# Row scales spread through memory, gates cumulated by a scan: a two-layer hybrid decoder on one core

## The chip, the core and the metric

The kernel runs on one core of a Trainium2 chip. The core's engines work side by side, each through its own list of instructions in order, and wait for each other on semaphores: TensorE (PE: matrix products and transposes into PSUM), VectorE (DVE), ScalarE (ACT), GpSimd (POOL) and SyncE (SP, which here only issues transfers). Transfers (DMA) are issued by SP, ACT or POOL and carried out by 16 DMA engines that these queues share. The metric is the device time of one execution in microseconds; lower is better.

## The reference

Two layers act on x of 256 rows by 1024. Each has three sub-layers, each with an RMS norm ahead and one behind it:

```python
def rms_norm(x, g):
    y = x * lax.rsqrt(jnp.mean(x * x, axis=-1, keepdims=True) + EPS)
    return y * g

for l in range(DEPTH):                          # 2
    h = rms_norm(x, pre_mix_g[l])
    x = x + rms_norm(parallel_mixer(h, ...), post_mix_g[l])
    h = rms_norm(x, pre_cross_g[l])
    x = x + rms_norm(memory_cross_attention(h, mem_n, ...), post_cross_g[l])
    h = rms_norm(x, pre_ffn_g[l])
    x = x + rms_norm((silu(h @ w_gate) * (h @ w_up)) @ w_down, post_ffn_g[l])
```

The mixer projects h by w_in (1024 x 3080) and gives the columns to three groups of heads: an RG-LRU (a gated linear recurrence), a forgetting attention (FoX, 8 heads) and a retention (4 heads). Of the FoX group this matters here: each head has a gate per row, and the logits take differences of the gates' running sum.

```python
log_f = jax.nn.log_sigmoid(f_logit + b_f)       # (rows, 8)
c = jnp.cumsum(log_f, axis=1).transpose(0, 2, 1)
logits = q @ k.T * scale + c[..., None] - c[:, :, None, :]
```

Cross-attention goes from the rows to 256 memory rows; the FFN is 2816 wide.

## The kernel before

The 256 rows are two tiles of 128 (`NT = 2`). Weights come in pieces of 512 KB: SP loads a piece into one of five `raw` buffers, ScalarE rounds it to `hi`, VectorE forms the rest `lo` = raw - hi, and PE computes every product three times (hi by hi, hi by lo, lo by hi). A raw buffer is free for the next load when `lo` is done. VectorE and ScalarE do this among their other work, in order.

A norm's gain goes into the transposed activations `xt` at once, but its 1 / rms (`rstd`, one number per row, computed on GpSimd as a power) is applied only to the products. Where a product has the rows on partitions, that is a scale per partition. Where it is transposed (columns on partitions, rows along the free axis: the mixer's `lru` and `fk` projections and the FFN's `gate` and `up`), the 256 numbers have to stand on every partition. The function `spread` makes this tile, `rsb`, once per mixer and once per FFN, four times in all: VectorE scales the identity by `rstd` (`diag`), PE multiplies a matrix of ones by that, ScalarE copies the result from PSUM. The users read `got["rs"]`: `lxp`, `lyT` and two `kT` in a mixer, the `fs` of nine pieces in an FFN.

In `gates`, the log gates `lf` (128 rows by 8, from a `softplus` on VectorE) are cumulated along the rows by three products with a triangle `tri` and with ones; the result `cT` (8 x 256) is written to memory by GpSimd's queue and read back four times, spread over all partitions (`far`).

Order: the kernel's code runs against a planner (`Flow`) with cost figures and a clock for each engine. Tasks are Python generators; a task that yields a tile goes on when the planner's PE clock has passed the time at which the tile is ready by its figures. So the order of each engine's instructions is fixed when the program is built, and a transfer's latency in the figures moves whatever waits for its tile to a later place in the lists. GpSimd's list holds, besides transfers (`PO.dma_start`: mask, constants, memory rows `msrc`, `cum`, `far`, and the post-norm gains `gpost`), the powers for the norms and, in layer 0, a chain of some 30 small operations for the rotary tables (`ang`). From these VectorE and ScalarE make `cs` and `c`, PE transposes them into `turn`, and the retention's `rot` needs `turn`.

The first FFN piece (`first`) has rows on partitions: gate, up, a product `fg` on VectorE, transposes on PE (`flip`), then the spread. The later pieces (`hidden`) are transposed ones. `summed` projects one piece into `fs`.

Of the kernel before, what the change touches and what calls it, by code (L numbers as in the profile page):

```python
# [10 lines left out]
F32 = mybir.dt.float32  # L11
# [4 lines left out]
ALU = mybir.AluOpType  # L16
AX = mybir.AxisListType.X

P = 128
D = 1024  # L20
KC = D // P
SEQ = 256
NT = SEQ // P
# [98 lines left out]
def _size(ap):  # L122
    return int(np.prod(ap.shape[1:]))
# [163 lines left out]
def decoder(ctx: ExitStack, tc: tile.TileContext, a, out):  # L287
    nc = tc.nc
    flow = Flow()
    V, S, PO = Engine(nc.vector, "DVE", flow), Engine(nc.scalar, "ACT", flow), Engine(nc.gpsimd, "POOL", flow)  # L290
# [6 lines left out]
    dp = ctx.enter_context(tc.tile_pool(name="dram", bufs=1, space=bass.MemoryType.DRAM))  # L297
# [5 lines left out]
    def nm(s):  # L303
        uid[0] += 1
        return f"{s}{uid[0]}"

    def work(shape, dt=F32, n="w"):
        return kp.tile(shape, dt, tag="w", name=nm(n), bufs=WORK_BUFS)
# [4 lines left out]
    def bank(n="ps"):  # L313
        return pp.tile([P, 512], F32, tag="ps", name=nm(n))
# [4 lines left out]
    def matmul(out_ap, lhsT, rhs, start, stop):  # L319
        nc.tensor.matmul(out_ap, lhsT, rhs, start=start, stop=stop)  # L320
        n = _size(out_ap)
        if lhsT.dtype == F32:
            cost = 2 * max(0.112, n / 1200.0 + 0.0025)
        elif lhsT.dtype == F32R:
            cost = max(0.119, n * 0.4475e-3 + 0.0025)
        else:
            cost = n / 2400.0 + 0.0025
        if lhsT.shape[0] == HD or out_ap.shape[0] == HD:
            cost *= 0.5
        elif lhsT.shape[0] == 32:  # L330
            cost *= 0.25
        flow.issue("PE", cost * flow.slow(), [out_ap], [lhsT, rhs])
# [6 lines left out]
    def transpose(out_ap, src):  # L339
        k = src.shape[0]  # L340
        nc.tensor.transpose(out_ap, src, ident[0:k, 0:k])  # L341
        flow.issue("PE", 0.109 * flow.slow(), [out_ap], [src])
# [37 lines left out]
    def half(ap, c):  # L380
        return ap[:, SEQ * c:SEQ * c + SEQ]

    def halves(ap, n=2):
        return ap.rearrange("p (c i) -> p c i", c=n)

    def transposes(src_list):

        b = bank("tr")
        for j, s in enumerate(src_list):
            transpose(b[0:s.shape[-1], j * P:(j + 1) * P], s)  # L390
        return b
# [25 lines left out]
    for l in range(DEPTH):  # L417
        b = {}
# [20 lines left out]
        for c in range(FB):  # L439
            c0, n = (0, 512) if c == 0 else (512 + SEQ * (c - 1), SEQ)  # L440
# [68 lines left out]
    def project(x, b):  # L509

        q = bank("acc")
        for k in range(KC):
            wh, wl = weights(b, k, NT)
            mm3(q[:, 0:b.n], x[0][:, k, :], x[1][:, k, :], wh, wl, k == 0, k == KC - 1)
            flow.tick()
        return q
# [17 lines left out]
    def project_w(x, b, c):  # L534


        q = bank("acc")
        for k in range(KC):
            wh, wl = weights(b, k, 2, slice(P * c, P * c + P))
            both = lambda: matmul(q.rearrange("p (s t i) -> p s t i", s=2, t=NT), wh, x[:, :, :, k, :], k == 0, k == KC - 1)  # L540
            if k == 0:
                both()
            matmul(halves(half(q, 0)), wl, x[:, 0, :, k, :], False, False)
            if k > 0:
                both()
            flow.tick()
        return q
# [14 lines left out]
    ident, tri, ones = (cst[:, c:c + P] for c in (C_ID, C_TRI, C_ONE))  # L562
# [213 lines left out]
    def spread(xt, got):  # L776

        while not all(n.scaled for n in xt):
            yield 0.3
        yield [n.rs for n in xt]  # L780
        d = work([P, NT, P], n="diag")
        for t in range(NT):
            V.tensor_scalar(d[:, t, :], ident, xt[t].rs, None, op0=ALU.mult)
        yield d
        b = bank("rsb")
        matmul(half(b, 0), ones, d.rearrange("p t i -> p (t i)"), True, True)
        rb = work([P, SEQ], n="rsb")
        S.copy(rb, half(b, 0))
        yield rb
        got["rs"] = rb  # L790

    def mixer(l, xt, blk, skew, between=None):
        mt = mixed()
        got = {}
        v = [work([P, 512], n="fv") for _ in range(NT)]
        rs = [None] * NT
# [4 lines left out]
        lf = [lfs[:, 4 + 8 * t:12 + 8 * t] for t in range(NT)]  # L801
# [24 lines left out]
        def gates():  # L826


            yield list(lf)
            b = bank("cum")  # L830
            matmul(b[0:8, 0:P], lf[0], tri, True, True)
            matmul(b[0:8, P:SEQ], lf[0], ones, True, False)
            matmul(b[0:8, P:SEQ], lf[1], tri, False, True)
            cT = work([8, SEQ], n="cT")
            V.tensor_copy(cT, b[0:8, 0:SEQ])
            yield cT
            dr = dp.tile([8, SEQ], F32, tag="cum", name=nm("cum"), bufs=2)
            PO.dma_start(out=dr, in_=cT)
            yield dr
            for e in range(2):  # L840
                for g in range(2):
                    far[e, g] = work([P, 2, SEQ], n="far")
                    PO.dma_start(out=far[e, g], in_=dr[4 * e + 2 * g:4 * e + 2 * g + 2, :].partition_broadcast(P))
            got["far"] = 1
# [266 lines left out]
    def parts(src, n):  # L1111

        h, l = work([P, 512], F32R, n=n + "h"), work([P, 512], F32R, n=n + "l")
        split(h, l, src)
        return h, l
# [63 lines left out]
    def ffn(xt, blk, make_post):  # L1179


        gt, got = {}, {}
        dn = [[None] * 2 for _ in range(NT)]

        def first():
            for t in range(NT):
                flow.need(lambda: xt[t].done)
                qg = project(xt[t].x, blk["gate", 0])
                tg, gg = work([P, 512], n="ft"), work([P, 512], n="fg")
                S.activation(tg, qg, AF.Tanh, bias=0.0, scale=xt[t].by[0.5])  # L1190
                V.scalar_tensor_tensor(gg, tg, 1.0, qg, op0=ALU.add, op1=ALU.mult)
                qu = project(xt[t].x, blk["up", 0])
                V.scalar_tensor_tensor(gg, gg, xt[t].rs, qu, op0=ALU.mult, op1=ALU.mult)
                flow.spawn(flip(t, gg), gg)
            flow.spawn(spread(xt, got))

        def flip(t, gg):
            tb = transposes([gg[:, j * P:(j + 1) * P] for j in range(4)])
            h, l = parts(tb, "g")
            for k in range(4):  # L1200
                gt[t, k] = tuple(x[:, k * P:(k + 1) * P] for x in (h, l))
            return
            yield

        def summed(b):

            w = work([P, 512], n="fs")
            for c in range(2):
                q = project_w(xt_all[2], b, c)
                S.copy(half(w, c), half(q, 1))  # L1210
                V.tensor_tensor(half(w, c), half(q, 0), half(w, c), op=ALU.add)
            return w

        def hidden(c):
            gs, tg = summed(blk["gate", c]), work([P, 512], n="ft")
            flow.need(lambda: "rs" in got)
            V.tensor_tensor(halves(gs), halves(gs), got["rs"].unsqueeze(1).to_broadcast([P, 2, SEQ]), op=ALU.mult)
            S.activation(tg, gs, AF.Tanh, bias=0.0, scale=0.5)
            V.scalar_tensor_tensor(gs, tg, 1.0, gs, op0=ALU.add, op1=ALU.mult)
            us = summed(blk["up", c])  # L1220
            V.tensor_tensor(gs, gs, us, op=ALU.mult)
            h, l = parts(gs, "g")
            for t in range(NT):
                for k in range(2):
                    o = SEQ * k + P * t
                    gt[t, 4 + 2 * (c - 1) + k] = tuple(x[:, o:o + P] for x in (h, l))

        def step(t, k, cc):
            if k == 0:
                dn[t][cc] = bank("dn")  # L1230
            flow.need(lambda: (t, k) in gt)
            wh, wl = weights(blk["down", k], 0, 2 * NT, slice(512 * cc, 512 * cc + 512))
            mm3(dn[t][cc], gt[t, k][0], gt[t, k][1], wh, wl, k == 0, k == FK - 1)
            flow.tick()

        first()
        spare.extend(range(NT))
        for c in range(1, FB):
            if c == FB - 1:
                spawn_post = make_post()  # L1240
            hidden(c)
            for k in blk["down_at", c]:
                for t in range(NT):
                    for cc in range(2):
                        step(t, k, cc)
        late = blk["down_at", FB]
        for t in range(NT):
            for k, cc in order(late):
                step(t, k, cc)
            spawn_post(t, dn[t], xt[t])  # L1250
        del spare[:]
# [66 lines left out]
    for l in range(DEPTH):  # L1318
        b = blks[l]
# [46 lines left out]
```

## Time and profile before

| | |
|---|---|
| median of 3 runs | 832.49 us (831.71 to 832.66) |
| the profiled execution, its own time | 832.4 us |
| its span in the trace | 830.6 us |
| granted TensorE clock | 0.998 |
| DVE, ACT, POOL busy | 71%, 54%, 10% |
| weights' queue q1 | 138.17 MB, 52.1% of the DMA engines' time |
| GpSimd's queue q0 | 7.91 MB, 2.8% |

A row of the timeline has the start, the duration, the engine, line and operation, the tile written and the tiles read (without buffer numbers) and a count; in brackets stands how long the engine had been idle before, and who ended that. Nearly all instructions carry the line of a helper (L242, L320), so they are told apart by tiles. A row of the chain that ended last has start, duration and what. Matmuls overlap, so their durations add up to more than the time; starts tell the time that each takes. A row of the table by stretches has the stretch, the sum of busy time, busy time and count of PE, PEld (weight loads), DVE, ACT and POOL, then the granted clock, the share in which the DMA engines were busy, and GB/s.

### The profile page before, as it was taken

Reading aid. Unit: us, or ns where it says so; the run is one execution under the profiler, and the core shown is the slowest. Engines: PE = TensorE matmul, PEld = TensorE weight load, DVE = VectorE, ACT = ScalarE, POOL = GpSimd, SP = SyncE. Lnnn points to the kernel's source line nnn. Section 1 sums busy time; section 2 is a strip of 40 time slices with the busy share of each in tenths; the row PEclk is TensorE's granted clock in tenths of the full one; section 3 lists DMA queues with packets and bytes.
Section 4 is the critical chain, followed back from the end, with each engine's and each line's share of the span. In section 5 each row is a group of like instructions: output and inputs, shape, how many; then the busy total and the mean of one; then the engine's idle time right before and its main releaser. Section 6 shows DMA issues by size and latency. Waiting matters only on the chain.

```text
span 830.6 us, 12999 instructions
## 1 busy us (share of the span) xinstructions
PE 818.8 (99%) x5023; PEld 714.9 (86%) x5023; DVE 588.9 (71%) x854; ACT 450.6 (54%) x728; POOL 80.2 (10%) x136
## 2 busy tenths in 40 slices
PE   9989999999999999999999999999999999999996
PEld 6989977998888888888889998789988788888885
DVE  6578996867577766758678888566767775857663
ACT  5569465746366544645474376555545563554541
POOL 2752100200020000000041100010002000000000
PEclk9999999999999999999999999999999999999999
DMA  8883545563357846557447563446444765647411
GB/s 296 305 260 121 171 158 155 188 216 114 121 185 240 251 138 220 186 157 232 137 128 237 168 204 127 151 129 228 145 129 133 232 222 181 207 147 244 139 49 51
DMA packets 101885, 147.50 MB, mean 178 GB/s; under 512 B 4976, under 2 KB 79104, under 8 KB 101696
## 3 DMA queue, kind: packets, MB, share of 16 engines
q1 hardware_dynamic: 99040, 138.17, 52.1%
q0 software_dynamic: 2080, 7.91, 2.8%
q8 instruction: 39, 0.64, 0.3%
q10 hardware_dynamic: 704, 0.59, 0.2%
q14 instruction: 22, 0.18, 0.1%
HBM read 145.59 MB, written 1.06 MB: 177 GB/s over the span
## 4 chain that ended last, share of the span: by engine, by line
PE 89%; DMA 3%; POOL 2%; issue 2%; DVE 2%; ACT 1%; DVEq 0%; POOLq 0%; ACTq 0%
PE acc L320 55%; PE dn L320 25%; PE tr L341 3%; DMA raw<-in_w_in 2%; PE co L320 1%; PE clg L320 1%; DMA raw<-in_w_down 1%; PE lg L320 1%; ACT hi L242 1%; POOL ang L242 1%; PE fo L320 1%; DVE lo L242 1%; PE ry L320 1%; POOL f L242 0%; PE gate L320 0%
## 5 line engine op out<-in xcount | busy, mean ns | idle before, releaser
L242 DVE TENSOR_TENSOR lo<-raw,hi 128x1024 fp32r<-128x1024 f32 (+2 forms) x246 | 293.9, 1215 | 88.1 <-ACT hi L242 86.7
L320 PE MATMUL acc<-xt,hi 128*128 128x256 f32 (+1 forms) x1344 | 340.1, 332 | 0.0
L242 ACT CAST hi<-raw 128x1024 fp32r<-128x1024 f32 (+2 forms) x246 | 251.9, 1043 | 92.5 <-PE acc L320 59.8
L320 PE MATMUL acc<-xt,lo 128*128 128x256 f32 x960 | 259.1, 282 | 0.0
L320 PEld LDWEIGHTS acc<-xt,hi 128*128 128x128 f32 x1344 | 223.3, 189 | 20.9 <-issue 0.4
L320 PEld LDWEIGHTS acc<-xt,lo 128*128 128x128 f32 x960 | 181.2, 189 | 6.3
L320 PE MATMUL acc<-hi,xt 128*128 128x512 f32 (+2 forms) x320 | 83.6, 351 | 0.0
L320 PEld LDWEIGHTS acc<-hi,xt 128*128 128x128 f32 x320 | 56.1, 188 | 8.5 <-ACT hi L242 0.6
L242 POOL TENSOR_TENSOR rp<-ssp,mh 128x1 f32<-128x1 f32 x12 | 6.8, 567 | 573.1 <-DVE ssp L242 573.0
L320 PE MATMUL acc<-lo,xt 128*128 128x512 f32 (+2 forms) x160 | 54.1, 349 | 0.0
L320 PE MATMUL dn<-hi,mth 128*128 128x512 f32 x128 | 51.6, 403 | 0.0
L242 DVE TENSOR_TENSOR fs<-acc,fs 128x256 f32<-128x256 f32 x72 | 30.1, 418 | 29.0 <-ACT fs L242 29.0
L320 PE MATMUL dn<-hi,mtl 128*128 128x512 f32 x128 | 50.5, 394 | 0.0
L320 PE MATMUL dn<-lo,mth 128*128 128x512 f32 x128 | 50.5, 394 | 0.0
L320 PE MATMUL acc<-mem,hi 128*128 128x256 f32 x256 | 47.3, 285 | 0.0
L242 ACT COPY fs<-acc 128x256 f32<-128x256 f32 x72 | 26.2, 364 | 37.7 <-PE acc L320 37.7
L320 PE MATMUL acc<-hi,mem 128*128 128x512 f32 x128 | 45.1, 405 | 0.0
L320 PE MATMUL dn<-hi,gh 128*128 128x512 f32 x112 | 44.3, 396 | 0.0
L320 PE MATMUL dn<-hi,gl 128*128 128x512 f32 x112 | 44.2, 394 | 0.0
L320 PE MATMUL dn<-lo,gh 128*128 128x512 f32 x112 | 44.2, 394 | 0.0
L320 PEld LDWEIGHTS acc<-mem,hi 128*128 128x128 f32 x256 | 39.5, 189 | 1.4 <-issue 1.0
L242 DVE TENSOR_TENSOR y<-dn,gpost 128x512 f32<-128x512 f32 x24 | 16.4, 685 | 28.3 <-ACT junk L242 28.3
(206 smaller groups left out, 1168.7 us busy)
## 6 DMA issues: line engine op xcount, KB each, us to landing
raw<-in_w_gate SPq DMA_DIRECT2D x44, 512.0 KB, 4.8
raw<-in_w_up SPq DMA_DIRECT2D x44, 512.0 KB, 4.6
raw<-in_w_down SPq DMA_DIRECT2D x44, 512.0 KB, 4.7
raw<-in_w_in SPq DMA_DIRECT2D x42, 512.0 KB, 5.4
raw<-in_w_ck SPq DMA_DIRECT2D x16, 512.0 KB, 3.7
raw<-in_w_cv SPq DMA_DIRECT2D x16, 512.0 KB, 4.9
raw<-in_w_out SPq DMA_DIRECT2D x16, 512.0 KB, 4.1
raw<-in_w_cq SPq DMA_DIRECT2D x16, 512.0 KB, 4.5
```

Source lines behind the costliest of these rows:

```text
L242: fn(*args, **kw)
L320: nc.tensor.matmul(out_ap, lhsT, rhs, start=start, stop=stop)
L341: nc.tensor.transpose(out_ap, src, ident[0:k, 0:k])
```

## The change

1. `spread`: each row tile's `rstd` (128 numbers of 4 bytes) is written to a tile `rs` in memory by GpSimd's queue, and one more transfer of that queue reads the 256 numbers back for every partition. `diag`, the product and the copy go.
2. `gates`: two transposes bring `lf` to 8 x 256 in PSUM, and a scan on VectorE over them with a tile of ones gives `cT`. The three products and the copy go.
3. `hidden`: where `rs` is not there yet by the planner, the `up` product is taken ahead of the gate's scaling.

```diff
@@ spread
-        d = work([P, NT, P], n="diag")
+        dr = dp.tile([NT * P, 1], F32, tag="rs", name=nm("rs"), bufs=2)
         for t in range(NT):
-            V.tensor_scalar(d[:, t, :], ident, xt[t].rs, None, op0=ALU.mult)
-        yield d
-        b = bank("rsb")
-        matmul(half(b, 0), ones, d.rearrange("p t i -> p (t i)"), True, True)
+            PO.dma_start(out=dr[t * P:(t + 1) * P, :], in_=xt[t].rs)
+        yield dr
         rb = work([P, SEQ], n="rsb")
-        S.copy(rb, half(b, 0))
+        PO.dma_start(out=rb, in_=dr[:, 0].partition_broadcast(P))
         yield rb
         got["rs"] = rb
@@ gates
             yield list(lf)
-            b = bank("cum")
-            matmul(b[0:8, 0:P], lf[0], tri, True, True)
-            matmul(b[0:8, P:SEQ], lf[0], ones, True, False)
-            matmul(b[0:8, P:SEQ], lf[1], tri, False, True)
-            cT = work([8, SEQ], n="cT")
-            V.tensor_copy(cT, b[0:8, 0:SEQ])
+            b = transposes(lf)
+            cT, one = work([8, SEQ], n="cT"), work([8, SEQ], n="one")
+            V.memset(one, 1.0)
+            V.tensor_tensor_scan(cT, one, b[0:8, 0:SEQ], 0.0, op0=ALU.mult, op1=ALU.add)
             yield cT
@@ hidden
             gs, tg = summed(blk["gate", c]), work([P, 512], n="ft")
+            us = None if "rs" in got else summed(blk["up", c])
             flow.need(lambda: "rs" in got)
...
-            us = summed(blk["up", c])
+            us = us or summed(blk["up", c])
             V.tensor_tensor(gs, gs, us, op=ALU.mult)
```

Three places in the lists, where the prediction's steps rest. First VectorE in layer 0, behind the softplus (`lo` is a weight piece, `lxp` and `lyT` use `rsb`, `ang` starts the end of the rotary tables). Before:

```order
L242 TENSOR_TENSOR lxp_647<-acc_584,rsb_528 128x2x256
L242 TENSOR_TENSOR lo_674<-raw_500,hi_673 128x1024
L242 COPY cT_681<-cum_677 8x256
L242 TENSOR_TENSOR lo_695<-raw_524,hi_694 128x1024
L242 TENSOR_TENSOR lo_712<-raw_557,hi_711 128x1024
L242 TENSOR_TENSOR lo_728<-raw_609,hi_727 128x1024
L242 TENSOR_TENSOR lyT_648<-acc_651,rsb_528 128x512
L242 TENSOR_TENSOR lo_757<-raw_645,hi_756 128x1024
L242 SCALAR_TENSOR_TENSOR ang_229<-ang_228 128x64
```

and now (the row of `cT` is the scan):

```order
L242 SCALAR_TENSOR_TENSOR cT_666<-one_667,tr_663 8x256
L242 TENSOR_TENSOR lo_686<-raw_524,hi_685 128x1024
L242 TENSOR_TENSOR lo_703<-raw_553,hi_702 128x1024
L242 TENSOR_TENSOR lo_721<-raw_603,hi_720 128x1024
L242 TENSOR_TENSOR lo_744<-raw_639,hi_743 128x1024
L242 MEMSET lxp_782 128x2x3
L242 TENSOR_TENSOR lxp_782<-acc_578,rsb_706 128x2x256
L242 TENSOR_TENSOR lyT_783<-acc_641,rsb_706 128x512
L242 TENSOR_TENSOR lo_800<-raw_655,hi_799 128x1024
L242 TENSOR_TENSOR mem_104<-xg_774,mem_104 128x512
L242 SCALAR_TENSOR_TENSOR ang_229<-ang_228 128x64
```

`lxp` moved behind two more `lo`, right ahead of `lyT`, and a part of `mem` (the memory's norm) came in ahead of `ang`.

Second GpSimd at the same time (`spl` ends its wait for the softplus, `ss` and `rstd` are the first memory tile's norm). Now:

```order
L242 TENSOR_SCALAR spl_81<-soft_83 128x4 x2
L242 TENSOR_SCALAR ang_230<-ang_226 128x64
L242 TENSOR_TENSOR ang_228<-ang_228,ang_230 128x64
L242 TENSOR_SCALAR ss_671<-ss_671 128x1
L242 TENSOR_TENSOR rstd_670<-ss_671,mh_78 128x1
L242 TENSOR_SCALAR ang_230<-ang_227 128x64
L242 TENSOR_TENSOR ang_228<-ang_228,ang_230 128x64
L237 DMA rsb_706<-rs_444 128x256
L242 TENSOR_SCALAR ang_230<-ang_226 128x64
L242 TENSOR_TENSOR ang_228<-ang_228,ang_230 128x64
L237 DMA cum_738<-cT_666 8x256
```

The read of `rsb` is new in it; the two writes of `rs` stand ahead of `spl`, and one pair of `ang` operations that was ahead of `spl` is now behind it.

Third GpSimd between the cross-attention and the FFN of layer 0 (`eps` is the last operation of the second row tile's norm). Now:

```order
L242 TENSOR_SCALAR eps_2825<-ss_2818 128x1
L237 DMA rs_2959<-rstd_2649 128x1
L237 DMA rs_2959<-rstd_2752 128x1
L237 DMA rsb_2980<-rs_2959 128x256
L237 DMA gpost_4165<-in_post_ffn_g 128x1024
```

Before, `gpost` stood right behind `eps`; now the three transfers of the spread stand between them. Layer 1 has the same.

## Prediction

> **What bounds the kernel.** I read the page's totals first, then the list of waits of TensorE (engine, tile and line that waited, for whom, us in total, times, longest), then the chain that ended last and the timeline at the places which the list names.
>
> ```profile
> span 830.6 us, 12999 instructions
> PE 818.8 (99%) x5023; PEld 714.9 (86%) x5023; DVE 588.9 (71%) x854; ACT 450.6 (54%) x728; POOL 80.2 (10%) x136
> ```
> ```profile
> PE cum L320 <- DVE hb L242: 1.5, 1, 1.5
> PE tr L341 <- DVE fg L242: 1.4, 2, 0.8
> PE warm L320 <- DVE warm L242: 1.2, 1, 1.2
> PE tr L341 <- DVE c L242: 1.0, 1, 1.0
> PE tr L341 <- ACT msrc L242: 0.4, 1, 0.4
> ```
>
> TensorE (PE) is busy 99% of the span, and all its waits for other engines are five kinds, 5.5 us. So a product taken from PE is worth its own time, except ahead of one of these waits: there PE only arrives sooner and waits longer. Three waits stand in layer 0 (cum, msrc, c), two in the heads of the FFNs (fg). The change touches both places.
>
> **Price of the removed products.** On PE's timeline I take start to start, since matmuls overlap.
>
> ```profile
> 34.83 0.28 PE L320 MATMUL acc<-xt,lo 128*128 128x256 f32 x1
> 34.95 0.60 PE L320 MATMUL rsb<-diag,cst 128*128 128x256 f32 x2
> 35.62 0.28 PE L320 MATMUL acc<-xt,lo 128*128 128x256 f32 x1
> ```
> ```profile
> 445.04 0.28 PE L320 MATMUL acc<-xt,lo 128*128 128x256 f32 x1
> 445.40 0.28 PE L320 MATMUL acc<-xt,lo 128*128 128x256 f32 x1
> 445.61 0.82 PE L320 MATMUL cum<-cst,soft 128*8 128x128 f32 x6
> 446.70 0.27 PE L320 MATMUL acc<-xt,lo 128*128 128x256 f32 x1
> ```
> ```profile
> 258.61 0.66 PE L341 MATMUL tr<-cst,fg 128*128 128x128 f32 x4 [0.60 <-DVE fg L242]
> 259.10 0.66 PE L320 MATMUL rsb<-diag,cst 128*128 128x256 f32 x2
> 259.72 0.39 PE L320 MATMUL acc<-xt,hi 128*128 128x512 f32 x1
> ```
> ```profile
> 69.94 0.44 PE tr L341 x4
> ```
>
> Three matmuls of 256 columns take 445.40 - 445.04 = 0.36 us, 0.12 each. The spread in a mixer costs 35.62 - 34.83 - 0.36 = 0.43 us. In the FFN the next "hi" would start one 0.12 us matmul after 259.10 and starts at 259.72: 0.50 us. The cumulation costs 446.70 - 445.40 - 0.36 = 0.94 us; two transposes at 0.44 / 4 each are 0.22, so 0.72 us is saved.
>
> Layer 1's mixer has no PE wait: gain 0.43 + 0.72 = 1.15 us. (GpSimd's wait for rs there holds only cum's write, which waits for cT anyway.) Both FFNs: 2 x 0.50 = 1.00 us.
>
> VectorE and ScalarE lose two diag scalings and a copy per spread; VectorE swaps a copy for a memset and a scan:
>
> ```profile
> L242 DVE COPY cT<-cum x2: 404/404/405, 51.6 to 447.7; 8x256 f32<-8x256 f32 x2
> L242 DVE TENSOR_TENSOR_SCAN ld<-t,li x4: 664/672/683, 93.8 to 494.5; 128x256 f32<-128x256 f32 x4
> ```
>
> A scan of 256 costs 0.27 us more than the copy, twice. I cost all this at nothing: these engines are 29% and 46% idle, and what waits for cT are far's loads, which the attention uses only after four more projections. Were that cover gone it would be 0.5 us.
>
> **Layer 0: three fixed times.** Here PE's gains are pinned.
>
> ```profile
> 47.70 0.81 PE L320 MATMUL cum<-cst,soft 128*8 128x128 f32 x6 [1.46 <-DVE hb L242]
> 48.79 0.28 PE L320 MATMUL acc<-xt,lo 128*128 128x256 f32 x1
> ```
> ```profile
> 54.41 0.57 POOL L242 TENSOR_TENSOR rstd<-ss,mh 128x1 f32<-128x1 f32 x1
> ```
> ```profile
> 56.22 0.66 PE L341 MATMUL tr<-cst,msrc 128*128 128x128 f32 x4 [0.36 <-ACT msrc L242]
> ```
> ```profile
> 57.13 1.23 DVE L242 TENSOR_TENSOR lo<-raw,hi 128x1024 fp32r<-128x1024 f32 x1 [2.90 <-ACT hi L242]
> 58.27 0.68 DVE L242 TENSOR_TENSOR lyT<-acc,rsb 128x512 f32<-128x512 f32 x1
> 60.22 0.22 DVE L242 SCALAR_TENSOR_TENSOR ang<-ang 128x64 f32<-128x64 f32 x1
> 60.99 0.50 DVE L242 COPY c<-cs 128x256 f32<-128x256 f32 x2 [0.32 <-ACT cs L242]
> ```
> ```profile
> 61.43 0.63 PE tr L341 x4
> ```
>
> The 0.43 us ahead of 47.70 goes into the wait for the softplus. From there PE is faster (0.22 us for 48.79 - 47.70 less two matmuls, 0.85), but the msrc transposes wait for GpSimd's rstd (ends 54.98) and ScalarE behind it, which the change does not move: still 56.22, with three matmuls fewer done (the order leaves 57 behind the cumulation instead of 60).
>
> Then the turn transposes. GpSimd issues the read of rsb two small operations after that rstd, at about 55.9. Its landing is unknown. The views of three tiles that go through the same queue, cT's write (8 KB), far's reads (256 KB each) and msrc's (512 KB), end with this row, and the list of DMA issues has posi's:
>
> ```profile
> DMA to landing us min/median/max: 2.3/3.2/4.0
> ```
> ```profile
> DMA to landing us min/median/max: 3.8/5.1/6.5
> ```
> ```profile
> DMA to landing us min/median/max: 7.6/8.8/10.1
> ```
> ```profile
> posi<-in_positions ACTq DMA_DIRECT2D x1, 1.0 KB, 5.3
> ```
>
> rsb has 128 KB of 1 KB rows, between cT's write and far's reads, and the DMA engines are busy here, so I take cT's 4.0 us: rsb lands at 59.9. VectorE has finished its two "lo" (57.13 plus 2 x 1.15, from the start-to-start step) at 59.4, so it waits 0.5 us in lxp; behind it in the order are lyT, a "lo" and a part of mem, 0.6 + 0.6 + 1.15 + 0.6, and only then ang: 62.85 instead of 60.22. c follows 0.77 and the transposes 0.44 later: 64.05. PE gets there at 56.22 + 0.44 + 21 x 0.12 + 0.44 + 33 x 0.12 = 63.6. So it waits 0.5 us instead of 1.0. By 64.05 it has done 21 matmuls and four transposes, 2.95 us, that before came after 61.43; that is ahead by 0.3 us: **layer 0 -0.3 us** out of 1.06 us saved. If rsb lands by 2.3 us, PE's own arrival limits it to -0.8; at far's 6.5 us it is +2.2.
>
> The write of 4-byte rows has no like in the trace; posi's 4-byte read took 5.3 us. It is issued ahead of GpSimd's own wait for the softplus, which ends when PE's does (47.70), and is needed at 55.9, so it is covered. The Trainium skill ("DMA: Bandwidth & Descriptors", Specifications) says transfers under 512 B are done as read-modify-write; no run here shows that yet.
>
> **FFN: the gain vector is loaded later.** GpSimd's queue now has rs, rs and rsb ahead of gpost, and rsb waits until both rs have landed.
>
> ```profile
> 243.86 0.62 POOL L237 DMA_DIRECT2D gpost<-in_post_ffn_g  x1
> ```
> ```profile
> q0 software_dynamic: 144, 0.52, 26.7%
> ```
> ```profile
> 248.00:252.00 4.00, 4.00 (x19) 3.23 (x18) 3.70 (x4) 3.61 (x4) 0.00 (x0) 1.00 0.78 238
> 252.00:256.00 4.00, 4.00 (x21) 3.37 (x20) 3.78 (x4) 2.52 (x3) 0.00 (x0) 1.00 0.90 274
> 652.00:656.00 4.00, 4.00 (x19) 3.31 (x18) 3.69 (x5) 3.35 (x4) 0.00 (x0) 1.00 0.54 162
> ```
> ```profile
> 250.32 5.17 DMA raw<-in_w_down
> ```
> ```profile
> 255.59 1.05 ACT L242 CAST hi<-raw 128x1024 fp32r<-128x1024 f32 x1 [0.97 <-DMA raw<-in_w_down]
> ```
>
> gpost itself is needed much later (the next post). But where it was issued at 243.86, now rs and rs are (the second at 244.5, 0.62 us each as gpost's own issue); with cT's quickest 2.3 us, since the weights' next load waits for a buffer then, they have landed at 246.8; rsb's issue takes another 0.6, and gpost goes at 247.4, 3.5 us later. Its data then fall into the stretch where w_down, issued at 250.32, lands at 255.49 and holds ScalarE's hi, VectorE's lo and fg behind it, and with fg PE's transposes (the 0.60 us wait). The DMA engines' work for gpost is 26.7% of the six-microsecond stretch 243 to 249: 1.6 us; rsb, a quarter of its bytes, 0.4. Until 255.5 they have 4 x 0.22 + 3.5 x 0.10 = 1.2 us free. What does not fit delays w_down and PE one for one: 2.0 - 1.2 = **0.8 to 0.9 us**, bounds 0 and 2.0. In layer 1 the same stretch is freer (0.54 in use from 652 to 656): there are 4 x 0.46 = 1.8 us free, of which I count three quarters, since the data begin about a microsecond into it, so I take **0.6 us**. Together +1.5. rsb itself is first used by VectorE behind the up sum now, a projection later than before, so it is there.
>
> **Sum.** -0.3 - 1.15 - 1.0 + 1.5 = -0.95 us against the profiled execution's 832.4 us (span 830.6), which stands 0.1 under the median 832.49: **831.5 us**. A measurement of this kernel tells about 0.2%, 1.66 us, from no change, so this counts as the same.
>
> **Rivals.**
> 1. The later gpost is hidden, since the engines have that room and w_down is ahead in its own queue. For it: 0.54 and 0.78 in use. Against: PE already waits for w_down, so nothing is left on that chain that could take up a delay. It gives 832.4 - 2.45 = 829.95; faster is decided once both delays together stay under 0.9 us.
> 2. The transfers take turns until gpost is done, and the free time is of no use. Then both delays are whole, 2 x 2.0: 832.4 - 2.45 + 4.0 = 833.95. The Trainium skill's page "DMA: Bandwidth & Descriptors" (Queues, rings and completion order) has each DMA engine go round-robin between queues by packets, which would make it so; the trace before never has both at work in the deciding stretch. Against it stands the free share in the rows above.
> 3. Slower: in layer 0 rsb lands as late as msrc did on the same queue under full DMA (7.6 at the least), and VectorE, in order, holds lo, ang and the turn behind lxp. Each microsecond past 4.0 costs one: 831.5 + 3.6 = 835.1. It decides above 6.7 us. Against it: rsb has a quarter of msrc's bytes and nothing large is ahead of it.
> 4. Other waits that the new order may bring in the mixers: the turn's users (rot, rsc) are nearer behind it than before. Unpriced; they fall under "slower".
>
> **Chances.** Forecast 0.42, rival 1 0.25, rival 2 0.13, rival 3 0.13, other waits 0.07. Faster by over 0.2%: rival 1 and a low edge of the forecast, 0.31. Slower: rival 3 and other waits, 0.20. Same: 0.49. The range from 829.7 to 834.6 leaves out rival 3, other waits and a little of rival 1.
>
> **What would show it.** PE's wait at the fg transposes near 258 and 663: 1.2 to 1.5 us if right, 0.6 under rival 1, over 2 under rival 2, with gpost issued 3 to 4 us later. The waits at cum 1.9, at msrc 1.3, at c 0.5. lxp idle under 1 us, over 3 under rival 3. Wrong altogether if PE shows waits in layer 1's mixer, or if rsb is late in an FFN.

## The result and the profile after

The changed kernel takes 853.69 us (851.96 to 854.05), before beside it 832.29 us: ratio 1.0261, 95% interval 1.0248 to 1.0273. It is 21.4 us slower; 831.5 was predicted. The profiled execution took 852.0 us. Its page, as at the head of the prediction:

```profile
span 850.2 us, 12967 instructions
PE 821.5 (97%) x5007; PEld 718.8 (85%) x5007; DVE 588.7 (69%) x848; ACT 448.3 (53%) x724; POOL 86.6 (10%) x148
```

The span grew by 19.6 us, and PE's busy time by 2.7 only. The rest stands in the list of PE's waits (line and tile that waited, for whom, us in total, times, longest):

```profile
PE tr L341 <- DVE fg L242: 12.5, 2, 6.8
PE tr L341 <- DVE hb L242: 6.9, 1, 6.9
...
PE tr L341 <- DVE c L242: 1.0, 1, 1.0
```

The fg transposes at the head of the two FFNs wait 12.5 us instead of 1.4, the transposes behind the softplus (`hb` is VectorE's last operation ahead of them) 6.9 instead of 1.5. That is 16.5 us. The chain that ended last tells why VectorE was late (start, duration, what), first in after, then at the place of its first row in before:

```profile
31.31 15.73 DMA raw<-in_w_in
448.19 11.04 DMA raw<-in_w_in
256.98 10.23 DMA raw<-in_w_down
667.42 11.06 DMA raw<-in_w_down
```

```profile
32.04 10.23 DMA raw<-in_w_in
```

In four places, one for each spread, the chain runs through a load of weights on SP's queue. The loads ahead of the fg transposes took 5.17 and 5.30 us in before. The change had touched neither that queue nor its loads. GpSimd's list in the first FFN (start, duration, operation, tiles; in brackets the idle time ahead of it):

```profile
250.38 1.18 POOL L237 DMA_DIRECT2D rs<-rstd  x2
260.61 0.55 POOL L237 DMA_DIRECT2D rsb<-rs  x1 [9.04 <-PE acc L320]
261.16 0.54 POOL L237 DMA_DIRECT2D gpost<-in_post_ffn_g  x1
```

The read of rsb had to wait until both writes of rs had landed; the bracket names PE, but the DMA issues of 247 to 257 us (tile, queue, KB each, median us from issue to landing) show the writes on the way:

```profile
raw<-in_w_down SPq DMA_DIRECT2D x3, 512.0 KB, 10.1
rs<-rstd POOLq DMA_DIRECT2D x2, 0.5 KB, 8.9
```

And the table by stretches (columns as in the prediction, the last one GB/s):

```profile
249.00:251.00 2.00, 2.00 (x10) 1.64 (x9) 0.75 (x1) 0.00 (x1) 1.74 (x5) 1.00 0.01 2
251.00:253.00 2.00, 2.00 (x12) 1.66 (x11) 0.46 (x1) 1.53 (x2) 0.57 (x2) 1.00 0.02 1
...
257.00:259.00 2.00, 2.00 (x10) 1.66 (x9) 1.88 (x3) 1.61 (x3) 0.00 (x0) 1.00 0.98 49
...
261.00:263.00 2.00, 2.00 (x13) 1.73 (x12) 0.00 (x0) 0.00 (x0) 0.70 (x2) 1.00 0.50 133
...
267.00:269.00 2.00, 0.00 (x0) 0.00 (x0) 1.59 (x2) 1.32 (x2) 0.00 (x0) 0.50 1.06 379
...
271.00:273.00 2.00, 2.00 (x9) 1.81 (x8) 0.69 (x1) 0.59 (x1) 0.00 (x0) 0.50 1.10 349
```

Two writes of 512 bytes are issued at 250.4, and for the ten microseconds after that next to nothing moves: 1 GB/s at 252, 49 at 258, where before moved 238 to 274 in this part of the FFN. At 258 the DMA engines count as busy all the same (0.98). PE goes on until the split weights are used up, then stands still. Its granted clock falls to 0.50 while it stands, and is still there for some microseconds afterwards. So PE, busy all through 271 to 273, has 9 matmuls at work there, where there were 13 from 261 to 263.

### The profile page after: what moved, and what is told of

Read it like the earlier page. It is cut to its first block, busy times and chain, and to the rows that moved or that the text cites. A ratio compares the mean times of both kernels' runs of the same rounds, so it can differ in the third digit from the quotient of the medians.

```text
span 850.2 us, 12967 instructions
## 1 busy us (share of the span) xinstructions
PE 821.5 (97%) x5007; PEld 718.8 (85%) x5007; DVE 588.7 (69%) x848; ACT 448.3 (53%) x724; POOL 86.6 (10%) x148
## 4 chain that ended last, share of the span: by engine, by line
PE 84%; DMA 7%; DVE 3%; POOL 2%; issue 2%; ACT 1%; DVEq 0%; POOLq 0%; SPq 0%; ACTq 0%
PE acc L320 51%; PE dn L320 24%; DMA raw<-in_w_in 3%; PE tr L341 3%; DMA raw<-in_w_down 3%; DVE lo L242 1%; PE co L320 1%; PE clg L320 1%; POOL ang L242 1%; PE lg L320 1%; ACT hi L242 1%; PE fo L320 1%; DMA rsb<-rs 1%; PE ry L320 1%; DMA x<-in_x 0%
## 5 line engine op out<-in xcount | busy, mean ns | idle before, releaser
L320 PE MATMUL acc<-xt,hi 128*128 128x256 f32 (+1 forms) x1344 | 344.7, 335 | 0.0
L320 PE MATMUL acc<-xt,lo 128*128 128x256 f32 x960 | 261.8, 285 | 0.0
L320 PEld LDWEIGHTS acc<-xt,hi 128*128 128x128 f32 x1344 | 227.1, 192 | 20.6
L320 PEld LDWEIGHTS acc<-xt,lo 128*128 128x128 f32 x960 | 184.3, 192 | 6.1
```

## Experiments

Theory W: the writes of 4-byte rows hold up the weight loads of the other queue. Its rival L: the spread's way through memory is long, and what stands behind it in the lists (rsb, the `up` sum taken ahead, gpost) comes late. Kernels named idle_ are before with transfers added at each spread that nobody reads, ahead of `diag`; apart from them each engine's list is that of before.

### Halves of the change, and other ways to write

**scan_only**

```diff
--- before
-            matmul(b[0:8, 0:P], lf[0], tri, True, True)
...
+            b = transposes(lf)
...
+            V.tensor_tensor_scan(cT, one, b[0:8, 0:SEQ], 0.0, op0=ALU.mult, op1=ALU.add)
```

> The gates' change alone: two transposes and the scan, with the spread by a product as before. Theory W (the writes of 4-byte rows hold up the weight loads of the other queue, about 5 us of PE's time for each of the four spreads) and theory L (the spread's way through memory is late, and what stands behind it in the lists with it) both put the loss into the spread: 831.3 to 832.5 us here. If the scan or its place on VectorE had a part in it, above 834.

830.53 us against 831.50, ratio 0.9991 (0.9982 to 1.0001), a little under the expected range: the scan takes no part in the loss.

**spread_only** (after, with the products of before for `cum`)

```diff
--- after
-            V.tensor_tensor_scan(cT, one, b[0:8, 0:SEQ], 0.0, op0=ALU.mult, op1=ALU.add)
...
+            matmul(b[0:8, 0:P], lf[0], tri, True, True)
```

> The spread's change alone, with the gates' running sum by products as before. Theories W and L both: the whole loss, 852 to 856 us, and PE's long waits at the fg transposes and at the softplus again. If the scan had a part in it: 836 to 848.

851.12 us, ratio 1.0234 (1.0217 to 1.0252), 0.9 us under the expected range: the loss is in the spread, as both theories have it.

**row_write**

```diff
--- after
...
-            PO.dma_start(out=dr[t * P:(t + 1) * P, :], in_=xt[t].rs)
+            transpose(b[0:1, t * P:(t + 1) * P], xt[t].rs)
+        row = work([1, SEQ], n="row")
+        V.tensor_copy(row, b[0:1, 0:SEQ])
+        yield row
+        dr = dp.tile([1, SEQ], F32, tag="rs", name=nm("rs"), bufs=2)
+        PO.dma_start(out=dr, in_=row)
...
```

> After, but with rstd turned by two PE transposes into one row of 256, copied by VectorE and written as one row of 1 KB, then read back over all partitions as after does; gpost still stands behind it in GpSimd's queue, and the up sum is still taken ahead. Theory W: the writes of 4-byte rows are gone, so the stall is, 831 to 836 us, with no wait over 3 us at the fg transposes. Theory L: the round trip is as long and the order is as in after, so 848 to 856.

829.22 us, ratio 0.9974 (0.9965 to 0.9983): not only is the loss gone, this is 2.3 us faster than before, and below the 831 to 836 that W had here. Its waits:

```profile
PE tr L341 <- DVE hb L242: 1.4, 1, 1.4
PE warm L320 <- DVE warm L242: 1.2, 1, 1.2
PE tr L341 <- ACT msrc L242: 1.1, 1, 1.1
PE tr L341 <- DVE c L242: 0.9, 1, 0.9
```

No wait is left at the fg transposes, though rsb makes the same detour (its read lands 4.6 to 6.3 us after its issue, 5.4 to 7.1 in after). Against L.

**idle_write**

```diff
--- before
+        dr = dp.tile([NT * P, 1], F32, tag="rs", name=nm("rs"), bufs=2)
+        for t in range(NT):
+            nc.gpsimd.dma_start(out=dr[t * P:(t + 1) * P, :], in_=xt[t].rs)
         d = work([P, NT, P], n="diag")
```

> Before, with the two writes of 128 4-byte rows added on GpSimd's queue at each spread, which nobody reads; the product stays, and each engine's list is otherwise before's. Theory W: 846 to 856 us, with idle time of PE at the same places as in after. Theory L: nobody waits for them, so 832 to 834.

858.44 us (851.98 to 859.76), ratio 1.0312 (1.0272 to 1.0352), above the 846 to 856 that W had here. The profiled execution is the 851.98; the other three took 858 to 860, and no trace shows where they spent the 6 to 8 us more. PE's two long waits are there again, though nobody reads what is written:

```profile
PE tr L341 <- DVE fg L242: 11.5, 2, 6.3
PE cum L320 <- DVE hb L242: 7.0, 1, 7.0
```

Where the time went shows in the starts of the same instructions (first and last of each group), in before and then in idle_write:

```profile
L237 POOL DMA_DIRECT2D gpost<-in_post_cross_g x2: 631/634/636, 163.7 to 568.7; - x2
L242 DVE TENSOR_TENSOR fs<-fs,rsb x18: 691/692/695, 264.9 to 802.8; 128x512 f32<-128x512 f32 x18
```

```profile
L237 POOL DMA_DIRECT2D gpost<-in_post_cross_g x2: 631/632/633, 169.5 to 581.4; - x2
L242 DVE TENSOR_TENSOR fs<-fs,rsb x18: 691/693/695, 276.8 to 822.3; 128x512 f32<-128x512 f32 x18
```

It is 5.8 us late behind layer 0's mixer (163.7 to 169.5), 11.9 at the first FFN's first `fs`, 12.7 behind layer 1's mixer, 19.5 at the last `fs`: about 6, 6, 1 and 7 us for the four spreads. In layer 1's mixer the loads stand as long, but PE works through (4.00 us busy in each 4 from 448 to 464 in after): there the split weights last. W holds; L, as the cause of the loss, is out.

### What makes the writes slow

W1: they all change the same 512 bytes. W2: each 4-byte write is slow. W3: the number of rows costs.

**idle_stride, idle_wide**

```diff
--- idle_write, for idle_stride
-        dr = dp.tile([NT * P, 1], F32, tag="rs", name=nm("rs"), bufs=2)
+        dr = dp.tile([NT * P, P], F32, tag="rs", name=nm("rs"), bufs=2)
-            nc.gpsimd.dma_start(out=dr[t * P:(t + 1) * P, :], in_=xt[t].rs)
+            nc.gpsimd.dma_start(out=dr[t * P:(t + 1) * P, 0:1], in_=xt[t].rs)
--- for idle_wide instead
+            nc.gpsimd.dma_start(out=dr[t * P:(t + 1) * P, :], in_=ident)
```

> As idle_write (the writes that nobody reads, added to before), but each of the 128 numbers goes to the head of its own 512 bytes of memory instead of side by side. Two forms of theory W: if the writes are slow because they all change the same 512 bytes, one after the other (W1), this is harmless, 832 to 837 us; if any 4-byte write is slow by itself (W2), 848 to 862 as idle_write.

> As idle_write, but each of the 128 rows is 512 bytes wide (a copy of the identity that nobody reads), so 64 KB per transfer. W1 and W2: whole 512 bytes are written at once, 832 to 836 us. If the number of rows is what costs (W3), 848 to 862.

831.65 us, ratio 0.9999 (0.9990 to 1.0008), and 832.24 us, 1.0008 (0.9998 to 1.0017). The same 256 writes of 4 bytes cost nothing once each has 512 bytes to itself: for W1, against W2 and W3. The issues of 240 to 270 us, idle_write, then idle_stride:

```profile
rs<-rstd POOLq DMA_DIRECT2D x2, 0.5 KB, 8.7
```

```profile
rs<-rstd POOLq DMA_DIRECT2D x2, 0.5 KB, 1.8
```

**idle_one** (`range(1)` for `range(NT)` in idle_write: one of the two writes)

> As idle_write, with the first row tile's write alone, half the dose. The DMA engines should stand about 5 us instead of 10, and PE lost about 5 to 6 of 10 at each spread, so the loads that are ahead cover about 4 to 5: W gives 832 to 842 us, less than half of idle_write's loss.

851.40 us, ratio 1.0241 (1.0226 to 1.0257): a miss. Half the writes cost 19.4 us, about as much as idle_write's profiled execution lost (851.98 against 831.50, 20.5 us).

```profile
rs<-rstd POOLq DMA_DIRECT2D x1, 0.5 KB, 8.8
```

One write takes as long as two side by side, which go to 512 bytes each. So the dose is not in the number of transfers.

**idle_quarter, idle_16b**

```diff
--- idle_write, for idle_quarter
+            nc.gpsimd.dma_start(out=dr[t * P:t * P + 32, :], in_=xt[t].rs[0:32, :])
--- for idle_16b instead
+        dr = dp.tile([NT * P, 4], F32, tag="rs", name=nm("rs"), bufs=2)
+            nc.gpsimd.dma_start(out=dr[t * P:(t + 1) * P, :], in_=ident[:, 0:4])
```

> As idle_write, but only the first 32 rows of each row tile are written (32 numbers of 4 bytes into the same 128 bytes). idle_one's one write took as long as idle_write's two side by side, so what counts is not the number of transfers. Theory W1 with a price for each write into the same 512 bytes, one after the other: 9.7 / 128 = 0.076 us each, so 2.4 us and a landing 3 to 5 us after the issue; the loads ahead cover it, 832 to 835 us. If the price is fixed, or belongs to pieces of 64 bytes that hold 16 numbers here as there: landing 8 to 10 us, 846 to 860.

> As idle_write, but each of the 128 rows has 16 bytes (four columns of the identity that nobody reads), side by side: 32 writes into each 512 bytes, four of these at a time. W1 as above: landing 3 to 5 us, 832 to 835. If each small write costs, whatever it shares its 512 bytes with: as idle_write, 848 to 862.

841.84 us, ratio 1.0125 (1.0106 to 1.0144), and 834.36 us, 1.0030 (1.0016 to 1.0044). idle_quarter is neither as W1 had it nor at the full price; idle_16b is within its range. Both have 32 writes in 512 bytes, and they differ by 7.5 us. In the first FFN, idle_quarter and then idle_16b:

```profile
rs<-rstd POOLq DMA_DIRECT2D x2, 0.1 KB, 3.5
```

```profile
rs<-cst POOLq DMA_DIRECT2D x2, 2.0 KB, 1.8
```

In the second FFN it was 5.6 and 2.1 us. What sets them apart is either that 16 bytes are enough, or that 4 instead of 16 writes share 64 bytes.

**idle_s16, idle_s64** (as idle_stride with `[NT * P, 4]` and `[NT * P, 16]`)

> As idle_write, but the 4-byte numbers stand 16 bytes apart (the places of idle_16b, with 4 of each 16 bytes written): 32 writes in each 512 bytes, 4 in each 64. idle_quarter, with 32 in 512 but 16 in 64, cost 10 us, idle_16b 2.9. If what counts is how many writes share 64 bytes (or fewer), this is as idle_16b: landing near 2 us in the FFN, 832 to 835 us. If it is how many 4-byte writes share 512 bytes, and rows of 16 bytes are whole pieces by themselves: as idle_quarter, landing 3.5 to 6 us in the FFN, 838 to 844.

> As idle_write, with the 4-byte numbers 64 bytes apart: 8 writes in each 512 bytes, one in each 64. By either count nearly free: landing 1.8 to 2.5 us in the FFN, 831 to 833.5 us. If it is a shared stretch longer than 512 bytes that counts: 838 or more.

834.08 us, ratio 1.0029 (1.0018 to 1.0039), and 831.90 us, 1.0000 (0.9991 to 1.0010). With 4 bytes in each 16, the time is idle_16b's and so is the landing (1.9 us in the first FFN, 2.1 in the second). So it is not the width of a write that counts (4 or 16 bytes at the same places), but how many fall close together:

| 4-byte or 16-byte writes | in 64 bytes | in 512 bytes | landing in the two FFNs, us | time against before, us |
|---|---|---|---|---|
| idle_write, 4 B | 16 | 128 | 8.7, 8.9 | +26.9 |
| idle_one, 4 B | 16 | 128 | 8.8, 8.6 | +19.4 |
| idle_quarter, 4 B | 16 | 32 | 3.5, 5.6 | +10.4 |
| idle_s16, 4 B | 4 | 32 | 1.9, 2.1 | +2.4 |
| idle_16b, 16 B | 4 | 32 | 1.8, 2.1 | +2.9 |
| idle_s64, 4 B | 1 | 8 | 1.8, 2.1 | +0.2 |
| idle_stride, 4 B | 1 | 1 | 1.8, 2.2 | -0.3 |

With 32 writes in 512 bytes in both, idle_quarter and idle_s16 differ by how many share 64 bytes, 16 or 4. Between idle_quarter and idle_write the number in 512 bytes and the number of writes in a transfer change together, so the table does not tell how the price is shared between these two. The landings are those of the FFNs; in the mixers the harmless writes too took 4.3 to 6.6 us (medians, idle_stride).

**idle_actq** (`nc.scalar` for `nc.gpsimd` in idle_write)

> As idle_write, but issued by ScalarE's queue. If the queue makes no difference (W), 846 to 862 us, with the weight loads again held up; if it is GpSimd's queue that makes the writes slow, 832 to 836.

838.57 us, ratio 1.0084 (1.0069 to 1.0100): between the two. The writes land as late (10.1 and 11.7 us in the FFNs), and layer 0's mixer loses as much (PE waits 7.6 us at `cum`), but in the FFNs PE waits 0.6 us in all. This is not because the weights are spared. In the first FFN the writes come at another time, and the loads beside them are held (the issue, then the issues of 262 to 274 us):

```profile
262.80 0.81 ACTq L783 DMA_DIRECT2D rs<-rstd  x2
```

```profile
raw<-in_w_up SPq DMA_DIRECT2D x2, 512.0 KB, 8.1
raw<-in_w_down SPq DMA_DIRECT2D x2, 512.0 KB, 9.4
raw<-in_w_gate SPq DMA_DIRECT2D x1, 512.0 KB, 8.2
rs<-rstd ACTq DMA_DIRECT2D x2, 0.5 KB, 10.1
```

In idle_write GpSimd issued them at 249.5 us, with the last w_down that fg needs still to come. ScalarE, in order, reaches them at 262.80, when that w_down has landed. In before the loads of 260 to 276 us took 4.1 to 4.4 us (medians); here those beside the writes take 8.1 to 9.4, and PE still works all through 266 to 276. In the second FFN the writes go out at 667.3, and w_up and w_down take 12.6 and 10.4 us beside them (664 to 680). So the slow writes hold SP's loads from ScalarE's queue too; what PE loses depends on the stretch that they hit.

### The prediction's own term: gpost issued later

**sbuf_row, sbuf_gpost**

```diff
--- row_write, for sbuf_row
...
-            transpose(b[0:1, t * P:(t + 1) * P], xt[t].rs)
...
-        V.tensor_copy(row, b[0:1, 0:SEQ])
+            PO.dma_start(out=row[0:1, t * P:(t + 1) * P], in_=xt[t].rs)
--- sbuf_row, for sbuf_gpost (in spread, behind the wait for the norms, FFNs only)
+        if ahead:
+            ahead()          # load_post("post_ffn_g", l)
```

> row_write without its two PE transposes and the copy: each row tile's 128 numbers go by 4-byte writes into one row of SBUF, side by side, and from there as one 1 KB row to memory and back over all partitions. If the stall belongs to writes into device memory: the writes land within 3 to 6 us, 827.5 to 831 us. If it belongs to small writes side by side into any memory: 846 to 858.

> sbuf_row with one change: gpost of the FFN is issued ahead of the spread's transfers on GpSimd's queue instead of behind them. sbuf_row lost 5.2 us, most of it in the first FFN, where gpost was issued at 251.2 us instead of 243.9 and its 512 KB moved in turns with w_down. If that is the price of the later gpost (the prediction had 0.9 us there), it goes: 831.5 to 834. If the loss is in rsb's read or in the lateness of the spread: 835.5 to 838.

sbuf_row 836.69 us, ratio 1.0066 (1.0051 to 1.0081): a miss, between the two expectations. Its 4-byte writes into SBUF land in 2.0 us in the first FFN. But gpost comes into the stretch where w_down is on its way (issues of 246 to 262 us):

```profile
251.17 0.54 POOL L237 DMA_DIRECT2D gpost<-in_post_ffn_g  x1
```

```profile
raw<-in_w_down SPq DMA_DIRECT2D x3, 512.0 KB, 7.2
...
gpost<-in_post_ffn_g POOLq DMA_DIRECT2D x1, 512.0 KB, 7.8
```

sbuf_gpost 832.17 us (830.51 to 840.00), 1.0018 (0.9996 to 1.0039): 4.5 us less. The fg transposes of the first FFN (eight of them: durations, first to last start), sbuf_row and then sbuf_gpost:

```profile
L341 PE MATMUL tr<-cst,fg x8: 271/347/477, 246.5 to 264.1; 128*128 128x128 f32 x8
```

```profile
L341 PE MATMUL tr<-cst,fg x8: 270/272/328, 245.9 to 259.7; 128*128 128x128 f32 x8
```

17.6 us from first to last against 13.8 (14.4 in before): behind the spread gpost costs 3.8 us there, where the prediction had 0.9. In sbuf_row's second FFN, where the prediction had 0.6, PE's wait at fg is 0.4 us: nothing of the kind shows.

**after_gpost** (the same edit on after)

> After, with gpost of the FFN issued ahead of the 4-byte writes. By theory W1 the writes hold the loads in any case: 849 to 856 us, PE's waits at the fg transposes 5 us and more. If a part of after's loss were the later gpost: less than after by that part, as large as in sbuf_row up to 4 us, 846 to 849.

852.53 us, ratio 1.0251 (1.0236 to 1.0266), an interval that overlaps after's. In after this term is not felt: while the writes hold everything, it does not matter what waits behind them.

### The two gains apart

**row_only** (row_write with the products of before for `cum`)

> row_write with the gates' products instead of the transposes and the scan, to part the two gains. row_write took 2.3 us less than before. If the scan is worth what the prediction has in layer 1 (0.7 us) and nothing in layer 0, 829.5 to 831 us. If all of row_write's gain is in the spread: the same as row_write, 829; if all is in the scan: 831 to 832.

830.96 us, ratio 0.9997 (0.9987 to 1.0006); with row_write's 0.9974 and scan_only's 0.9991 each half alone is within what the measurement tells from no change, and only both together are outside it. By the starts of the same matmuls in the traces, layer 1's mixer gains 0.9 us in row_write, 0.8 in scan_only and 0.3 in row_only, so the scan is worth 0.6 to 0.8 there; each FFN gains 1.0 to 1.3 in row_write and row_only. But 0.4 to 0.5 of that is also there in scan_only, which leaves the FFN as it was, and where the wait at fg shrinks from 1.4 to 0.5 us.

## Why the prediction was wrong

By the starts of the same matmuls in the traces, us against before (the forecast by its own terms):

| | forecast | after | row_write |
|---|---|---|---|
| layer 0, mixer | -0.3 | +6.7 | +0.3 |
| layer 0, FFN | +0.4 | +6.0 | -1.0 |
| layer 1, mixer | -1.15 | -0.8 | -0.9 |
| layer 1, FFN | +0.1 | +7.7 | -1.2 |

1. **What bounds the kernel: right.** PE was 99% busy, and the whole loss appears as PE's waits and the slow clock behind them.
2. **The step that failed** is the sentence on the write: it "has no like in the trace; posi's 4-byte read took 5.3 us", is needed at 55.9 and "so it is covered", and in the FFN "with cT's quickest 2.3 us" it "landed at 246.8". Measured: landings of 8.4 to 11.9 us, 8.9 in the first FFN. The nearest rows were a read of 4-byte numbers and a write of 1 KB rows, and I used them as ends of a range, though neither puts many writes into a few bytes; no row bounded it from above. Worse, I only asked whether the result would be back in time. The cost lies in what the write does to others: 512 bytes a transfer held the 512 KB loads beside them for some ten microseconds (10.1 us instead of the 4.5 of before in the same ten microseconds, 247 to 257). idle_write shows it with no reader at all.
3. **Products and scan: right in size.** Predicted 0.72 us for the cumulation in layer 1; 0.6 to 0.8 by the traces. The scan takes 0.27 us longer than the copy, as forecast, and hides. In the FFNs the product was 0.50 us; row_write gains 1.0 to 1.3 although it adds two transposes, since the wait at fg (1.4 us in both together) goes as well.
4. **The later gpost: right as a mechanism, wrong in size, and absent here.** 3.8 us in sbuf_row's first FFN instead of 0.9, above even rival 2's 2.0. It was issued at 251.2 there, so all its 512 KB moved beside w_down, which landed after 7.2 us instead of 4.4 in sbuf_gpost (246 to 262 us). The sum over free time let w_down have all that it needed, and this row does not bear that out. The Trainium skill's rule of turns by packets ("DMA: Bandwidth & Descriptors", Queues, rings and completion order), behind rival 2, fits this row better. In row_write gpost goes only at 264.6 and costs nothing, as in rival 1, but for another reason: it has left the deciding stretch altogether.
5. **Layer 0: rsb at 4.0 us** took 5.5 there in after (5.4 to 7.1 in all four places). The path behind it is right: the chain that ended last goes from its read (60.94, 5.46 us) through lxp, lyT, a lo, mem and ang to the turn's transposes, and PE waits 1.0 us for c, where 0.5 was forecast. Three waits were named as those that pin the gains, but the first of them, which I had treated as fixed, grew from 1.5 to 6.9 us through a load.
6. **Rivals.** None was a mechanism in which the spread's own transfers slow the weights. Rival 3 had the late rsb, but not its cause; VectorE's idle time ahead of lxp was 1.9 us, under the 3 that it asked for.
7. **The Trainium skill's rule on short transfers** ("DMA: Bandwidth & Descriptors", Specifications: under 512 bytes a read-modify-write) was set aside as seen in no run. The runs show that it is not the length alone: 4 bytes alone in 512 land in 1.8 us, like whole 512-byte rows (1.9 us). If read-modify-write is the cause, its price comes from writes to one place that wait for each other. That fits the table and is not shown; nor is it shown by what the writes hold the loads of another queue.

## What to carry to other kernels

Turn a column of numbers into a row on the chip before it is written to memory: 128 writes of 4 bytes side by side took 9 us and stopped the weight stream, one 1 KB row took 5 and stopped nothing. Price a new transfer by what it does to the transfers beside it, not only by whether its own data are back in time, and where the trace has nothing of its kind, leave the upper end open and give that a chance. A load that an inserted wait pushes into the stretch where the stream of weights is short costs microseconds; issue it ahead of the wait, or far behind it.

## What was not expected of the hardware

- 128 writes of 4 bytes into 512 contiguous bytes landed after 8.5 to 12.9 us from GpSimd's queue in idle_write and idle_one, whether one such transfer or two (to 512 bytes each) were under way; with a step of 64 bytes or more 1.7 to 6.9 us. Into one row of SBUF they landed in 2.0 us in the first FFN, where those with a step of 64 bytes took 1.8.
- In that time, in after's first FFN, the loads of another queue took 10 us instead of 4.5, and all queues together moved 1 to 49 GB/s. From ScalarE's queue the writes were as slow, and the loads beside them took 8.1 to 9.4 us.
- In after's three long waits (6.9, 5.7 and 6.8 us) the granted clock fell to 0.50 about 2.6, 2.0 and 4.7 us after PE's last matmul, and was back at 1.00 some 10, 7 and 7 us after the fall. The Trainium skill ("TensorE: Matmul & The Clock Gate", What's actually happening) gives half the clock after an idle window of about 3.4 us. Half the clock agrees; two of the three falls came sooner than that.
